# LayerNorm's mean product moved to the middle of a block of weight products; the last factors of the first 96 tokens in a PSUM bank of their own and multiplied first

## The chip, the core and the metric

The kernel runs on one core of one Trainium2 chip. The metric is the device time of one execution in microseconds. Three runs of the kernel before took 1078.56, 1078.71 and 1078.87 us, so the median is 1078.71 us.

A core has a matrix engine (PE in the profile, with its weight loads listed apart as PEld), three engines that work on elements (DVE, ACT, POOL), and an engine SP that here only issues transfers. Transfers are issued from the instruction streams ("queues") of SP, ACT and POOL. Every engine runs its own stream in order. An engine waits for another through semaphores. Products are written to PSUM, an accumulator memory divided into banks. Everything else lives in SBUF.

## What is computed

One layer of a decoder step for T = 288 tokens: 256 of a new sequence and 8 x 4 of running ones. The model width is D = 2048. Cut to what matters:

```
h   = rmsnorm(x)                       # 288 x 2048
a, gate, z = split(h @ w_in + b_in)    # three times 1024
c   = depthwise_conv31(a * sigmoid(gate)) + conv_b
c   = silu(layernorm(c) * ln_g + ln_b) # mean and variance over 1024
p   = (pooled(z) @ pool_w) * pool_scale
x   = x + concat(c, p) @ w_out
x   = x + relu(rmsnorm(x) @ w_ff1)**2 @ w_ff2    # width 8192
y   = rmsnorm(x)                       # the output
```

## The kernel before

Channels lie on the 128 partitions and tokens along the free dimension. A matrix product is cut into blocks of two output tiles of 128 channels, each 288 tokens wide in a PSUM tile `ac` with two banks. Because single matmuls run on rounded float32 values, each operand is split in a high part and a low part, and three of the four part products are taken. One block of `w_out` over eight input tiles (1024 inputs) is 8 x 2 x 3 = 48 matmuls.

The raw weights arrive in tiles `wr` of 128 x 1024 by transfers from SP. ACT writes the high part `whi` (L273). The low part `wlo` is the difference of raw and high part, taken by POOL in two pieces of 128 x 512 each (L281), or by DVE (L277), as a table says. For the `w_out` blocks it is POOL, for the later feed-forward blocks DVE. There are five buffers each for `whi` and `wlo`, so a cast L273 waits until PE has used up an earlier tile.

`gemm` (L309) issues the matmuls of a block; L304 is the one line that records every matmul. Its argument `between` names a function that is called at a given place among them: key `0` is ahead of the first matmul, key `4` is ahead of the pair of input tiles 4 and 5, which is half way through a block of eight. Its argument `classes` takes a string, `TURN`, by which the 48 matmuls of a block are put in another order; none is added or left out.

The pooling half of `w_out` runs first, in eight blocks g = 0 to 7 (L624 to L631). After each, DVE adds the result to `xT` (L631). Meanwhile DVE finishes the convolution's taps (L478), and then LayerNorm of the convolution's half is worked in between:

- `ln_mean` (L601): ACT copies a partial sum (L604), DVE adds the last tile to it (L605), and one PE product with a matrix of 1/1024 gives the mean in the PSUM tile `pmean`. It is called ahead of block g = 4.
- `ln_sums` (L608): DVE subtracts the mean from the four tiles `c` (L611, one operand in PSUM), ACT squares them (L613), DVE adds the four squares (three L617, then L618, all operands in SBUF). `by_parts` (L247) then splits the sum: ACT casts its high part (L251), DVE takes the low part into `hl` (L252), and PE multiplies both parts with a constant matrix. The result is the PSUM tile `norm`. It is called ahead of block g = 6.

Where no dependence forces an order, a scheduler decides where on each engine an instruction stands in the stream, from its own estimate of the times. It is not known from the program text alone.

At the end, the sum of squares of the final x is turned into one factor per token (L756 to L764). Three small products with an identity matrix spread 96 tokens each over all partitions (L767), once into the bank `ends` (`rows_f`) for DVE and once into `again`, which ACT copies to SBUF (`rf`, L779) for POOL. `finish` (L771) multiplies `xT` by the factors: DVE in six pieces of 1, 1, 2, 2, 3 and 3 tiles of 288 tokens, POOL in four pieces of one tile (L775). A transfer of each finished piece to the output follows at once (L776), in turn from SP and ACT.

The bank `idle` takes the results of three products that nothing reads (L759). They only keep PE running.

Of the kernel before, what the change touches and what calls it, by code (L numbers as in the profile page):

```python
# [12 lines left out]
ALU = mybir.AluOpType  # L13
# [3 lines left out]
P = 128  # L17
# [3 lines left out]
T = SEQ + NB * NS  # L21
TB = T // 3
# [47 lines left out]
TURN = "110100" * 4 + "01" * 6 + "1100" * 3  # L70
# [16 lines left out]
def trunk_kernel(ctx: ExitStack, tc: tile.TileContext, io):  # L87
# [3 lines left out]
    nc = tc.nc  # L91
# [14 lines left out]
    def nm(s):  # L106
        seen[s] = seen.get(s, 0) + 1
        return f"{s}{seen[s]}"
# [8 lines left out]
    def row(name):  # L117
        return rowp.tile([P, T], F32, name=nm(name), tag="row")
# [32 lines left out]
    xT = const.tile([P, KT, T], F32, name="xT")  # L151
# [63 lines left out]
    ident = const.tile([TB, TB], F32, name="ident", padded_shape=[TB, TB + 40])  # L215
# [85 lines left out]
    def mm(*args, **kw):  # L301

        with tc.issue_after(chain[-1]) if chain else nullcontext():
            last = nc.tensor.matmul(*args, **kw)  # L304
        if chain:
            chain[0] = last.ins
        return last

    def gemm(banks, rhs, added=None, m_outer=False, between={}, classes="", by_part=False, gets=None, pairs=None, late=0):  # L309


        n = len(rhs)
        gets = gets or ready.pop(0)
        todo, begins = [], {}
        if by_part:
            for k in range(0, n, 2):
                sets = [range(len(banks))] if k else [range(2), range(2, len(banks))]
                for last, ms_ in enumerate(sets, 1 - len(sets)):
                    for part, (w, x) in enumerate(((0, 0), (1, 0), (0, 1))):
                        if last == 0:  # L320
                            begins[len(todo)] = (k, None, k + 1)[part]
                        todo += [(k + (1 - d if x else d), m, w, x) for m in ms_ for d in range(2)]
        else:
            pairs = pairs or [(k, m) for k in range(0, n, 2) for m in range(len(banks))]
            if m_outer:
                pairs.sort(key=lambda km: km[1])
            for k, m in pairs:
                begins[len(todo)] = (k, m) if m else k
                todo += [(k + d, m, w, x) for d, w, x in ((0, 0, 0), (1, 0, 0), (0, 1, 0), (1, 1, 0), (1, 0, 1), (0, 0, 1))]
        todo[:late] = sorted(todo[:late], key=lambda p: p[2])  # L330
        head = todo[: len(classes)]
        for j, c in enumerate(classes):
            todo[j] = next(p for p in head if c == "." or (p[0] + p[3]) % 2 == int(c))
            head.remove(todo[j])
        if added:
            todo += [(n, 1, None, x) for x in range(2)]
        ends = {m: [f(j for j, p in enumerate(todo) if p[1] == m) for f in (min, max)] for m in range(len(banks))}
        ahead = None
        for j, (k, m, w, x) in enumerate(todo):
            if begins.get(j) in between:  # L340
                ahead = between[begins[j]]()
            with tc.issue_after(ahead.ins) if ahead is not None and not chain else nullcontext():
                last = mm(banks[m][:, :T], unit if w is None else gets[k // 8](k % 8, m)[w], added[x] if w is None else rhs[k][x], start=j == ends[m][0], stop=j == ends[m][1])
        ready.extend(itertools.islice(weights, 1))
        return last.ins

    def bank2():
        return acc.tile([P, 2, 512], F32, name=nm("ac"), tag="ac")

    def each(bk):  # L350
        return [bk[:, m, :] for m in range(2)]

    def halves(x2):

        return [(x2[0][:, m, :], x2[1][:, m, :]) for m in range(2)]
# [228 lines left out]
    proj = [halves(dd[k // 2])[k % 2] for k in korder]  # L584
# [34 lines left out]
        norm["rows"], last = row_of_sums(ssc[:, 0, :], "norm2", None, float(DC) / D, AF.Silu, parts=True)  # L619
        return last  # L620

    BETWEEN = {4: {0: ln_mean}, 6: {0: ln_sums}}
    behind = nullcontext()
    for g in range(8):  # L624
        bk = bks[g] if g < 2 else bank2()
        if g > 1:
            with behind:
                last = gemm(each(bk), proj, between=BETWEEN.get(g, {}), classes=TURN if g in (4, 6) else "")
        behind = tc.issue_after(last) if g > 3 else nullcontext()
        x2 = xT[:, 2 * g : 2 * g + 2, :]  # L630
        nc.vector.tensor_tensor(x2, x2, bk[:, :, :T], op=ALU.add)  # L631

    mixc = []
    for j, c in enumerate(cs):
        n = tmpp.tile([P, 2, T], F32, name=nm("n"), tag="ag", bufs=2)
# [17 lines left out]
    for g in range(8):  # L653
        bk = bks[g] if g < 2 else bank2()
        if g > 1:
            last = gemm(each(bk), mixc, classes=TURN if g == 2 else "")
# [14 lines left out]
        for m, (ah, al) in enumerate(a2):  # L671
            k = 2 * g + m
            xk = xT[:, k, :]
# [22 lines left out]
    for ch in range(DFF // FCH):  # L696
        fx, done = [], []
# [4 lines left out]
        for g in range(FCH // 256):  # L702
            bk = bank2()
# [4 lines left out]
            if ch or g:  # L708
# [9 lines left out]
                done = []  # L718
        last = ch == DFF // FCH - 1
        for g in range(8):  # L720
            bk = bank2()
# [7 lines left out]
            for m in range(2):  # L729
                k = 2 * g + m  # L730
                xk = xT[:, k, :]
# [19 lines left out]
    ends, again = ms("ends"), cvp.tile([P, 512], F32, name="again", tag="cv")[:, :T]  # L751
    sums_f, rows_f = ends[:TB, 0, 0:3], ends[:, 1, :T]
    idle = cvp.tile([P, 512], F32, name="idle", tag="cv")
    for n, (part, busy) in enumerate(((ssf, 0), (qf, 3))):
        for j in range(3):
            last = nc.tensor.matmul(sums_f[:, j : j + 1], part[:, j * TB : (j + 1) * TB], mean_d[:, 0:1], start=n + j == 0, stop=n == 1 and j == 2)  # L756
        with tc.issue_after(last.ins):
            for j in range(busy):
                nc.tensor.matmul(idle[:, 0:P], ones, ones, start=True, stop=True)  # L759
    root, first, s_f = [cst[:TB, 2 + 3 * j : 5 + 3 * j] for j in range(3)]  # L760
# [3 lines left out]
    nc.vector.scalar_tensor_tensor(out=s_f, in0=root, scalar=1.5, in1=first, op0=ALU.add, op1=ALU.mult)  # L764
    for spread_f in (rows_f, again):
        for j in range(3):
            nc.tensor.matmul(spread_f[:, j * TB : (j + 1) * TB], s_f[:, j : j + 1].to_broadcast([TB, P]), ident, start=j == 0, stop=j == 2)  # L767
    rf = row("rf")
    queues = (nc.sync, nc.scalar)

    def finish(eng, r, pieces):  # L771

        for j, (k0, n) in enumerate(pieces):
            xk = xT[:, k0 : k0 + n, :]
            eng.tensor_tensor(xk, xk, r[:, None, :].to_broadcast([P, n, T]), op=ALU.mult)  # L775
            queues[j % 2].dma_start(io["yT"][:, k0 : k0 + n, :], xk)  # L776

    finish(nc.vector, rows_f, ((0, 1), (1, 1), (2, 2), (4, 2), (6, 3), (9, 3)))
    nc.scalar.copy(rf, again)  # L779
    finish(nc.gpsimd, rf, [(k, 1) for k in range(12, KT)])  # L780


# [56 lines left out]
```

## Time and profile before

| | us |
|---|---|
| three runs: lowest, median, highest | 1078.56, 1078.71, 1078.87 |
| the profiled execution | 1078.44 |
| its span, first to last instruction | 1076.7 |
| PE busy | 1066.2 |
| DVE, ACT, POOL busy | 628.2, 482.2, 180.0 |

The profile is of one execution. Its span is 1.7 us shorter than its time; that rest lies outside the first and last instruction. A row of its timeline gives the start from the span's begin, the duration, the engine, the line and the operation, `out<-in` by the program's names, the shapes and a count when equal neighbours are merged (the duration then reaches from the first start to the last end). In brackets stands how long the engine was idle before, and what ended that. A name like SPq or ACTq is the engine's queue issuing a transfer. Matmuls are pipelined: two that follow each other at 0.13 us have a duration of 0.29 us each, and overlap.

### The profile page before, as it was taken

To read this page: it belongs to the slowest core of one execution; us is meant where nothing else is said; L and a number is where in the kernel's file an instruction comes from. 1 tells how busy PE (TensorE), PEld (TensorE's weight loads), DVE (VectorE), ACT (ScalarE), POOL (GpSimd) and SP (SyncE) were. 2 spreads that over 40 slices of the span, in tenths; PEclk is the share of its full clock that TensorE was granted. 3 is DMA by queue.
4 is the path that set the end of the run, shared out by engine and by line. 5 is a ranking of instruction groups with operands and counts; after the bars stand their busy time and mean duration, and the time that the engine had idled before them with its cause. 6 is when DMAs were issued, how large, how long until landed. Compare 5 with 4: busy or idle time off the path is not lost.

```text
span 1076.7 us, 19546 instructions
## 1 busy us (share of the span) xinstructions
PE 1066.2 (99%) x8176; PEld 1065.5 (99%) x8176; DVE 628.2 (58%) x799; ACT 482.2 (45%) x598; POOL 180.0 (17%) x192
## 2 busy tenths in 40 slices
PE   9999999999999999999999999999999999999996
PEld 9999999999999999999999999999999999999996
DVE  8899998878554544445554444455444445554553
ACT  8655654755544433334443333444433334444441
POOL 0989889423000000000000000000000000000001
PEclk9999999999999999999999999999999999999998
DMA  9897777555455555555545555555555555455522
GB/s 333 292 248 217 223 183 244 178 174 170 164 174 165 171 172 164 174 164 169 175 165 170 170 166 175 167 166 176 162 172 171 165 174 169 164 176 162 172 80 89
DMA packets 58873, 192.81 MB, mean 179 GB/s; under 512 B 6304, under 2 KB 11296, under 8 KB 58784
## 3 DMA queue, kind: packets, MB, share of 16 engines
q1 hardware_dynamic: 56336, 184.35, 52.6%
q0 software_dynamic: 1584, 5.77, 2.9%
q8 instruction: 64, 1.05, 0.4%
q10 hardware_dynamic: 864, 1.44, 0.4%
q14 instruction: 25, 0.20, 0.1%
HBM read 187.25 MB, written 4.28 MB: 178 GB/s over the span
## 4 chain that ended last, share of the span: by engine, by line
PE 79%; issue 20%; POOL 0%; DVE 0%; POOLq 0%
PE ac L304 78%; PE pp L304 1%; PE warm L214 1%; POOL xT L775 0%; POOLq L825 0%; DVE xT L748 0%; PE norm L304 0%; PE pmean L304 0%; PE mean L304 0%; DVE ones L204 0%; DVE cst L232 0%; POOLq L775 0%; DVE cst L231 0%
## 5 line engine op out<-in xcount | busy, mean ns | idle before, releaser
L273 ACT CAST whi<-wr 128x1024 fp32r<-128x1024 f32 (+1 forms) x332 | 346.4, 1043 | 541.5 <-PE ac L304 524.6
L277 DVE TENSOR_TENSOR wlo<-wr,whi 128x1024 fp32r<-128x1024 f32 x282 | 346.2, 1228 | 349.3 <-ACT whi L273 349.2
L304 PE MATMUL ac<-ax,whi 128*128 128x288 f32 x2048 | 351.1, 292 | 0.0
L304 PE MATMUL ac<-fx,whi 128*128 128x288 f32 x2048 | 350.2, 292 | 0.0
L304 PEld LDWEIGHTS ac<-ax,whi 128*128 128x128 f32 x2048 | 296.0, 187 | 0.0
L304 PEld LDWEIGHTS ac<-fx,whi 128*128 128x128 f32 x2048 | 295.7, 187 | 0.0
L304 PE MATMUL ac<-ax,wlo 128*128 128x288 f32 x1024 | 217.4, 292 | 0.0
L304 PE MATMUL ac<-fx,wlo 128*128 128x288 f32 x1024 | 216.4, 292 | 0.0
L304 PEld LDWEIGHTS ac<-ax,wlo 128*128 128x128 f32 x1024 | 162.6, 187 | 0.0
L304 PEld LDWEIGHTS ac<-fx,wlo 128*128 128x128 f32 x1024 | 162.3, 187 | 0.0
L775 POOL TENSOR_TENSOR xT<-xT,rf 128x288 f32<-128x288 f32 x4 | 3.1, 791 | 786.6 <-ACT rf L779 786.6
L304 PE MATMUL ac<-hx,whi 128*128 128x288 f32 x768 | 130.1, 293 | 0.0
L304 PEld LDWEIGHTS ac<-hx,whi 128*128 128x128 f32 x768 | 110.6, 187 | 0.2
L281 POOL TENSOR_TENSOR wlo<-wr,whi 128x512 fp32r<-128x512 f32 x78 | 104.3, 1394 | 19.9 <-ACT whi L273 17.4
L478 DVE SCALAR_TENSOR_TENSOR pc<-u_all,vec,pc 128x256 f32<-128x256 f32 x232 | 99.3, 481 | 5.0 <-ACT pc L475 3.6
L304 PE MATMUL ac<-hx,wlo 128*128 128x288 f32 x384 | 79.5, 292 | 0.0
L304 PEld LDWEIGHTS ac<-hx,wlo 128*128 128x128 f32 x384 | 60.3, 187 | 0.1
L304 PE MATMUL ac<-dx,whi 128*128 128x288 f32 x256 | 45.9, 294 | 0.0
L304 PE MATMUL ac<-mx,whi 128*128 128x288 f32 x256 | 44.5, 292 | 0.0
L711 DVE SCALAR_TENSOR_TENSOR t<-ac,r 128x576 f32<-128x576 f32 x32 | 24.2, 757 | 25.4 <-PE ac L304 25.3
L304 PEld LDWEIGHTS ac<-dx,whi 128*128 128x128 f32 x256 | 38.1, 188 | 0.1
L304 PEld LDWEIGHTS ac<-mx,whi 128*128 128x128 f32 x256 | 37.4, 187 | 0.0
(142 smaller groups left out, 541.8 us busy)
## 6 DMA issues: line engine op xcount, KB each, us to landing
wr<-in_w SPq DMA_DIRECT2D x335, 512.0 KB, 3.6
wlo<-in_w POOLq DMA_DIRECT2D x11, 512.0 KB, 9.3
xT<-in_xT SPq DMA_DIRECT2D x8, 288.0 KB, 7.3
wr<-in_w SPq DMA_DIRECT2D x5, 256.0 KB, 4.0
out_u_out<-u_all SPq DMA_DIRECT2D x1, 1208.0 KB, 8.9
u_all<-in_hist_c SPq DMA_DIRECT2D x8, 136.0 KB, 5.5
out_z_out<-z_all SPq DMA_DIRECT2D x1, 668.0 KB, 8.6
z_all<-in_hist_p SPq DMA_DIRECT2D x4, 152.0 KB, 6.9
```

The lines of the kernel that those rows point to most:

```text
L214: nc.tensor.matmul(warm[:, 0, 0:P], ones, ones, start=True, stop=True)
L273: nc.scalar.copy(hi, raw)
L277: nc.vector.tensor_tensor(lo, raw, f32(hi), op=ALU.subtract)
L281: nc.gpsimd.tensor_tensor(lo[:, j : j + 2, :], raw[:, j : j + 2, :], f32(hi[:, j : j + 2, :]), op=ALU.subtract)
L304: last = nc.tensor.matmul(*args, **kw)
L478: nc.vector.scalar_tensor_tensor(out=dst, in0=up[:, w : w + SEQ], scalar=cwv[:, w : w + 1], in1=pc, op0=ALU.mult, op1=ALU.add)
L711: nc.vector.scalar_tensor_tensor(out=t, in0=bk[:, :, :T], scalar=0.0, in1=both(rows2[0]), op0=ALU.max, op1=ALU.mult)
L775: eng.tensor_tensor(xk, xk, r[:, None, :].to_broadcast([P, n, T]), op=ALU.mult)
```

## The change

There are two edits.

In the `w_out` blocks, `ln_mean` is called at key 4 of block g = 4 in place of key 0, so its product stands behind 24 matmuls of that block. The order `TURN` is used for block 5 in place of block 4. Block 6 keeps it.

At the end, the product that spreads the first 96 tokens' factors goes to columns of the bank `idle` (`ahead_f`), not to `ends`. DVE multiplies these 96 tokens of four tiles first, then the other 192 tokens of the first pieces, then the 96 tokens of eight more tiles, then the rest. The transfers carry the same pieces from the same queues as before.

```diff
-    BETWEEN = {4: {0: ln_mean}, 6: {0: ln_sums}}
+    BETWEEN = {4: {4: ln_mean}, 6: {0: ln_sums}}
...
-                last = gemm(each(bk), proj, between=BETWEEN.get(g, {}), classes=TURN if g in (4, 6) else "")
+                last = gemm(each(bk), proj, between=BETWEEN.get(g, {}), classes=TURN if g in (5, 6) else "")
...
+    ahead_f = idle[:, P : P + TB]
...
     for spread_f in (rows_f, again):
         for j in range(3):
-            nc.tensor.matmul(spread_f[:, j * TB : (j + 1) * TB], s_f[:, j : j + 1].to_broadcast([TB, P]), ident, start=j == 0, stop=j == 2)
+            out = ahead_f if j == 0 and spread_f is rows_f else spread_f[:, j * TB : (j + 1) * TB]
+            nc.tensor.matmul(out, s_f[:, j : j + 1].to_broadcast([TB, P]), ident, start=j == 0 or out is not ahead_f and j == 1 and spread_f is rows_f, stop=j == 2 or out is ahead_f)
...
-    def finish(eng, r, pieces):
-
-        for j, (k0, n) in enumerate(pieces):
-            xk = xT[:, k0 : k0 + n, :]
-            eng.tensor_tensor(xk, xk, r[:, None, :].to_broadcast([P, n, T]), op=ALU.mult)
-            queues[j % 2].dma_start(io["yT"][:, k0 : k0 + n, :], xk)
-
-    finish(nc.vector, rows_f, ((0, 1), (1, 1), (2, 2), (4, 2), (6, 3), (9, 3)))
+    def times(eng, r, k0, n, t0=0):
+
+        xk = xT[:, k0 : k0 + n, t0 : t0 + r.shape[1]]
+        return eng.tensor_tensor(xk, xk, r[:, None, :].to_broadcast([P, n, r.shape[1]]), op=ALU.mult)
+
+    def finish(eng, r, pieces, t0=0, j0=0):
+
+        for j, (k0, n) in enumerate(pieces, j0):
+            done = times(eng, r, k0, n, t0)
+            queues[j % 2].dma_start(io["yT"][:, k0 : k0 + n, :], xT[:, k0 : k0 + n, :])
+        return done.ins
+
+    times(nc.vector, ahead_f, 0, 4)
+    last = finish(nc.vector, rows_f[:, TB:], ((0, 1), (1, 1), (2, 2)), TB)
+    with tc.issue_after(last):
+        times(nc.vector, ahead_f, 4, 8)
+    finish(nc.vector, rows_f[:, TB:], ((4, 2), (6, 3), (9, 3)), TB, 1)
```

PE's stream around the mean product, before: `ac_2473` is the result of block 3, `ac_2537` that of block 4, `dx_...` are the pooling half's inputs.

```order
 L304 MATMUL ac_2473<-dx_2119,wlo_2400 128x288 x2
 L304 MATMUL ac_2473<-dx_2119,whi_2399 128x288 x2
 L304 MATMUL pmean_2538<-sum_c,ones 128x288
 L304 MATMUL ac_2537<-dx_1242,whi_2462 128x288
 L304 MATMUL ac_2537<-dx_1242,wlo_2463 128x288
```

The same product in PE's stream now:

```order
 L304 MATMUL ac_2537<-dx_1582,wlo_2463 128x288 x2
 L304 MATMUL ac_2537<-dx_1582,whi_2462 128x288 x4
 L304 MATMUL ac_2537<-dx_1582,wlo_2463 128x288 x2
 L304 MATMUL ac_2537<-dx_1582,whi_2462 128x288 x2
 L304 MATMUL pmean_2562<-sum_c,ones 128x288
 L304 MATMUL ac_2537<-dx_1921,whi_2467 128x288 x2
 L304 MATMUL ac_2537<-dx_1921,wlo_2468 128x288 x2
```

It stands behind the block's first two input tile pairs (`dx_1242` and `dx_1582`), 24 matmuls later; the two products `norm` stay ahead of block 6.

DVE's stream from the last subtraction of the mean to `hl`; `ac_2537` is the result of block 4:

```order
-L611 TENSOR_TENSOR c_1716<-c_1716,pmean_2538 128x576
+L611 TENSOR_TENSOR c_636<-c_636,pmean_2562 128x576
+L611 TENSOR_TENSOR c_719<-c_719,pmean_2562 128x576
+L611 TENSOR_TENSOR c_1018<-c_1018,pmean_2562 128x576
+L611 TENSOR_TENSOR c_1716<-c_1716,pmean_2562 128x576
 L617 TENSOR_TENSOR q_2671<-q_2671,q_2674 128x576
+L631 TENSOR_TENSOR xT<-xT,ac_2537 128x576
 L617 TENSOR_TENSOR q_2671<-q_2671,q_2678 128x576
 L617 TENSOR_TENSOR q_2671<-q_2671,q_2682 128x576
 L618 TENSOR_TENSOR q_2671<-q_2671 128x288
-L631 TENSOR_TENSOR xT<-xT,ac_2537 128x576
 L252 TENSOR_TENSOR hl_2687<-q_2671,hl_2687 128x288
```

The addition of block 4's result (L631) has moved from behind L618 to between the first and the second addition of squares. The L611 rows differ only in the number of their tile.

ACT's stream over the same stretch; `whi_2599` belongs to block 6, `whi_2658` and `whi_2663` to block 7:

```order
 L273 CAST whi_2594<-wr_2590 128x1024
+L273 CAST whi_2599<-wr_2592 128x1024
 L613 ACTIVATE q_2671<-c_636 128x576
 L613 ACTIVATE q_2674<-c_719 128x576
 L613 ACTIVATE q_2678<-c_1018 128x576
-L273 CAST whi_2599<-wr_2592 128x1024
+L273 CAST whi_2658<-wr_2654 128x1024
 L613 ACTIVATE q_2682<-c_1716 128x576
-L273 CAST whi_2658<-wr_2654 128x1024
+L273 CAST whi_2663<-wr_2656 128x1024
 L251 CAST hl_2687<-q_2671 128x288
-L273 CAST whi_2663<-wr_2656 128x1024
```

Each of the three casts now stands one step of LayerNorm earlier. POOL's and SP's streams have the same rows in the same order as before, but for line numbers.

DVE's last rows now, in the place of six L775 rows on `ends` (two each of 128x288, 128x576 and 128x864):

```order
+L776 TENSOR_TENSOR xT<-xT,idle 128x4x96
+L776 TENSOR_TENSOR xT<-xT,ends_11504 128x192 x2
+L776 TENSOR_TENSOR xT<-xT,ends_11504 128x2x192
+L776 TENSOR_TENSOR xT<-xT,idle 128x8x96
+L776 TENSOR_TENSOR xT<-xT,ends_11504 128x2x192
+L776 TENSOR_TENSOR xT<-xT,ends_11504 128x3x192 x2
```

Two more rows read the first tokens' factors from `idle`, and the six rows on `ends` are 192 tokens wide per tile, not 288.

## The prediction

> **What bounds the kernel now.** I read the page first, then the chain of work that ended last, then PE's waits.
>
> ```profile
> span 1076.7 us, 19546 instructions
> PE 1066.2 (99%) x8176; PEld 1065.5 (99%) x8176; DVE 628.2 (58%) x799; ACT 482.2 (45%) x598; POOL 180.0 (17%) x192
> ...
> 188.56 0.51 PE pmean L304 x2
> 189.08 12.58 PE ac L304 x96
> 201.66 0.26 PE norm L304 x2
> 201.92 76.63 PE ac L304 x588
> ...
> PE ends L767 <- DVE cst L764: 0.2, 1, 0.2
> ```
>
> PE is busy for 1066.2 of 1076.7 us. From the first weights to the last block it waits for nothing: the list of its waits has one entry at the start and this one of 0.2 us in the tail. In the stretch that the change touches, the chain is PE from end to end: the mean product (two passes), blocks 4 and 5 (96 matmuls), the two `norm` products, and on. So whatever keeps PE waiting there is added to the time in full, and no other engine's work there can be shortened to any gain. Only the tail, where PE is through, can give something back.
>
> **The moved product itself.** It costs the same 0.51 us wherever it stands. Was it late before?
>
> ```profile
> 187.81 0.46 DVE L605 TENSOR_TENSOR sum_c<-pmean,c 128x288 f32<-128x288 f32 x1
> 188.60 0.75 DVE L631 TENSOR_TENSOR xT<-xT,ac 128x576 f32<-128x576 f32 x1 [0.34 <-PE ac L304]
> 189.27 2.74 DVE L611 TENSOR_TENSOR c<-c,pmean 128x576 f32<-128x576 f32 x4
> 191.93 3.91 DVE L617 TENSOR_TENSOR q<-q,q 128x576 f32<-128x576 f32 x3
> 195.88 1.43 DVE L618 TENSOR_TENSOR q<-q 128x288 f32<-128x288 f32 x1
> 197.23 0.74 DVE L631 TENSOR_TENSOR xT<-xT,ac 128x576 f32<-128x576 f32 x1
> 197.90 0.88 DVE L252 TENSOR_TENSOR hl<-q,hl 128x288 fp32r<-128x288 f32 x1
> ...
> 201.49 0.29 PE L304 MATMUL norm<-hl,means 128*128 128x288 f32 x1
> ```
>
> Its input L605 is done at 187.81 + 0.46 = 188.27, just ahead of its turn, and PE shows no wait. So the move takes away no stall: gain 0. Its other instructions, the copy L604 and L605, stand where they stood, and it issues no transfer. The order `TURN` goes from block 4 to block 5. Blocks 4 and 5 took 12.58 us for 96 matmuls, 0.131 each, against 76.63 / 588 = 0.130 later, so `TURN` costs under 0.1 us in either place. That the 24 matmuls behind the product now run in plain order is not in this trace; by the same two rates it is between 0 and 0.02 us.
>
> What changes is the time left behind it. Before, `hl` was ready at 197.90 + 0.88 = 198.78, and the first `norm` product ran at 201.49: 2.7 us to spare. The product now comes 24 x 0.13 = 3.1 us later, while `norm` keeps its place. **The slack is smaller than the delay**, so the chain from mean to `hl` has to be worked through.
>
> **How long that chain takes.** The rows for DVE above are uneven: L617 takes 0.76 us once and over 1.2 us twice, and L618, half as wide, takes 1.43. Single rows of DVE beside those of POOL show why.
>
> ```profile
> 191.32 1.28 POOL L281 TENSOR_TENSOR wlo<-wr,whi 128x512 fp32r<-128x512 f32 x1
> 191.93 1.28 DVE L617 TENSOR_TENSOR q<-q,q 128x576 f32<-128x576 f32 x1
> 193.32 0.76 DVE L617 TENSOR_TENSOR q<-q,q 128x576 f32<-128x576 f32 x1
> 193.52 1.70 POOL L281 TENSOR_TENSOR wlo<-wr,whi 128x512 fp32r<-128x512 f32 x1 [0.93 <-POOL wlo L281]
> 194.18 1.66 DVE L617 TENSOR_TENSOR q<-q,q 128x576 f32<-128x576 f32 x1
> 195.19 1.81 POOL L281 TENSOR_TENSOR wlo<-wr,whi 128x512 fp32r<-128x512 f32 x1
> 196.95 1.51 POOL L281 TENSOR_TENSOR wlo<-wr,whi 128x512 fp32r<-128x512 f32 x1
> ```
>
> POOL's piece ends at 192.60 and L617 0.61 later; the next pair ends at 195.22 and 195.84, 0.62 later. L618 ends 0.31 behind POOL's 197.00, and L252 0.32 behind its 198.46. The one L617 that found POOL idle took 0.76, and there POOL's piece was the longer one. So a DVE operation with both operands in SBUF and a POOL piece take turns. L611 and L631 read PSUM and keep 0.75 us throughout. The Trainium skill, "SBUF — State Buffer", section "SBUF: two separate sides", says it so: DVE with two SBUF inputs and GpSimd share a port pair, and whichever starts first holds it for its whole instruction. The rows agree.
>
> Now the chain is set on its new times. It needs ACT's rows, because POOL's pieces follow the casts.
>
> ```profile
> 192.34 1.05 ACT L273 CAST whi<-wr 128x1024 fp32r<-128x1024 f32 x1 [0.21 <-PE ac L304]
> 193.29 0.69 ACT L613 ACTIVATE q<-c 128x576 f32<-128x576 f32 x1
> 195.49 1.05 ACT L273 CAST whi<-wr 128x1024 fp32r<-128x1024 f32 x1 [1.52 <-issue]
> 197.34 0.43 ACT L251 CAST hl<-q 128x288 fp32r<-128x288 f32 x1 [0.80 <-DVE q L618]
> ```
>
> - The mean is there at 189.07 + 3.12 = 192.2. Four L611 (2.74) end at 194.9.
> - The cast at 192.34 waits for the first half of block 4, which now runs ahead of the product, 0.51 and a few hundredths earlier: 191.76. POOL began 193.52 - 192.34 = 1.18 behind the cast: now 192.94, and two pieces of 1.28 end at 195.5.
> - The first L617 is issued at 194.9 and loses its turn: 195.5 + 0.62 = 196.1.
> - L631, now second, ends at 196.1 - 0.08 + 0.75 = 196.77 (successors start 0.08 ahead of an end, as 197.23 against 197.31). The second L617 is issued at 196.69.
> - The cast at 195.49 waits for the end of block 4, which comes up to 0.1 earlier without `TURN`: 195.40. POOL's next piece begins 1.18 later: 196.58. The fourth L613 now stands behind this cast and ends by 195.40 + 1.05 + 0.69 = 197.1, in time for the third L617.
>
> So POOL would begin 0.1 us ahead of the second L617. **If POOL wins that turn**, its piece ends at 197.86 and L617 at 198.48. From there they alternate as before, when POOL's ends lay 1.78 (195.22 to 197.00) and 1.46 us (to 198.46) apart: POOL 199.64, third L617 200.26; POOL 201.42, L618 201.73; the cast L251 with 0.43 until 202.2; POOL 202.88, L252 at 203.20. The second `norm` product was due at 201.49 + 0.13 = 201.62. With 0.1 for handing over, PE waits 203.30 - 201.62 = **1.7 us**. This is also the worst of its kind: all five of DVE's operations then wait for the last five pieces that POOL has in this stage.
>
> Nothing hides this wait: PE runs in order, and block 6 is queued behind `norm`. What follows from `norm` shifts along with it.
>
> **The tail.** Which wait ends last there?
>
> ```profile
> 1066.00 0.91 PE L767 MATMUL ends<-ident,cst 96*128 96x96 f32 x6 [0.22 <-DVE cst L764]
> L775 DVE TENSOR_TENSOR xT<-xT,ends 128x576 f32<-128x576 f32 x2 | 1.4, 746 | 0.0
> L775 DVE TENSOR_TENSOR xT<-xT,ends 128x288 f32<-128x288 f32 x2 | 0.8, 450 | 1.0 <-PE ends L767 1.0
> 1066.94 0.46 DVE L775 TENSOR_TENSOR xT<-xT,ends 128x288 f32<-128x288 f32 x1 [1.00 <-PE ends L767]
> 1067.43 0.35 SPq L776 DMA_DIRECT2D out_yT<-xT  x1
> GB/s 0 0 0 0 0 0 0 0 0 0 0 0 0 0 0 0 0 0 0 173 377 182 412 374 423 396 366 447 407 363 445 401 407 347 41 11 0 0 0 0
> ```
>
> The last row cuts 1060 to 1077 into 40 slices of 0.425 us. The transfers run near 400 GB/s for all but two slices, the first (173) and the third (182). The end is bound by 16 x 144 KB of output, and only an earlier start and these gaps are to be had: at 400 GB/s, 0.24 + 0.23 us. One of three spreading products now lets DVE begin: two passes of 0.91 / 6 on, with the first start, near 1066.5, not 1066.94. The multiplication of 4 x 96 tokens is not in the trace: it lies between 450 ns (288 elements) and 746 (576), by the line between them 550. A 192-token piece is by the same line near 350. The first transfer is then issued at 1066.5 + 0.55 + 0.35 - 0.08 = 1067.3, against 1067.43: 0.1 us earlier. The third piece comes 0.4 earlier, but the 8 x 96 tokens (by the line 0.95 us) then delay the fourth by 0.3 and open a gap there. Together I take 0.2 us, with bounds of 0 and 0.5.
>
> **Sum.** The profiled execution took 1078.44; + 1.7 - 0.2 = 1079.9. The median of the three runs lies 0.27 above it, so the forecast for a median is **1080.2 us**, 1.5 us or 0.14% slower. A measurement of this kernel tells apart from no change about 0.2%, 2.2 us, so this counts as no difference.
>
> **Rivals.** First: DVE wins the turn at 196.7. The start of a row need not be the moment at which the port is taken:
>
> ```profile
> 127.19 1.89 POOL L281 TENSOR_TENSOR wlo<-wr,whi 128x512 fp32r<-128x512 f32 x1
> 127.23 0.70 DVE L524 SCALAR_TENSOR_TENSOR d<-s,z_all 128x512 f32<-128x512 f32 x1
> 231.54 0.91 POOL L682 TENSOR_TENSOR ss<-ss,q 128x288 f32<-128x288 f32 x1
> 231.70 1.06 DVE L675 SCALAR_TENSOR_TENSOR ax<-xT,vec,ax 128x288 fp32r<-128x288 f32 x1
> ```
>
> With a lead of 0.04 POOL lost and was stretched to 1.89; with 0.16 it won. The lead of 0.1 lies between. By the skill's rule above, POOL wins with any lead, which the first pair contradicts. If DVE wins, L617 ends at 197.45, POOL 1.15 later (as 195.22 behind 194.08) at 198.60, and the same alternation gives `hl` at 202.2: a wait of 0.7 us, a median of 1079.2.
>
> Second: the chain fits after all, for one POOL piece less in the way. Then only the tail is left: 1078.5. Against it: without any turn lost behind the first, the chain would still take three L617 or L631 of 0.75, 0.45 for L618 and a cast.
>
> Third, on the slower side: the wait lets PE's clock drop.
>
> ```profile
> 1070.00:1071.00 1.00, 0.00 (x0) 0.00 (x0) 1.00 (x2) 0.00 (x0) 1.00 (x2) 1.00 1.06 396
> 1071.00:1072.00 1.00, 0.00 (x0) 0.00 (x0) 0.02 (x1) 0.00 (x0) 0.15 (x1) 0.63 1.08 411
> ```
>
> The third number from the right is the granted clock: full up to 1071, more than 3 us after the last spreading products, then falling. A wait of 1.7 us is about half of that, so the point is not reached. If it were, a clock at half for some 3.4 us would add 1.7 (an estimate): 1081.9. "TensorE: Matmul & The Clock Gate" of the Trainium skill, part 1, gives an idle window of about 3.4 us, free-running; the rows agree that the drop comes after more than 3 us.
>
> **How the numbers follow.** POOL wins the turn, 0.50: 1079.8 to 1080.6. DVE wins it, 0.28: 1078.8 to 1079.5. No wait, 0.10: 1078.2 to 1078.8. The clock drops or something else unseen is late, 0.10: 1081 to 1083. A gain by a path that I do not see, 0.02. Faster by over 0.2% would need 2.2 us where only the tail's 0.5 is to be had: 0.02. Slower by over 0.2% is 0.12, the fourth case and the edge of the first. The range is 1078.5 to 1080.9.
>
> **What would show it.** Right: PE waits on `norm` for DVE's `hl`, 0.7 or 1.7 us; L617 and L618 end 0.6 and 0.3 behind POOL's pieces; DVE's first multiplication near 1066.5 plus the wait. Wrong: no wait of PE at `norm`, `hl` ready before 201.6, or another order of POOL and DVE at the second L617.

## The result and the profile after

| | median, us | lowest, us | ratio to before, with its 95% interval |
|---|---|---|---|
| before (14 executions) | 1078.86 | 1078.44 | |
| changed (14 executions) | 1080.76 | 1080.14 | 1.0018 [1.0011, 1.0025] |
| changed, second set (11) | 1081.26 | 1080.20 | 1.0016 [1.0007, 1.0025] |

The change makes the kernel slower by some 0.17%, about 1.8 us. One execution of the first set took 1252.14 us at a granted clock of 0.79; the ratio leaves it out, and without it that set's median is 1080.57. Both intervals lie above 1, and they are narrower than the 0.2% that the forecast took as the resolution: the loss is small, but it is measured. The profile after is of an execution of the second set, of 1080.93 us with a span of 1079.2 us.

PE's list of waits in the changed kernel (us in total, times, longest), without the 1.1 us at the start that both kernels have:

```profile
PE norm L304 <- ACT hl L251: 0.6, 1, 0.6
PE norm L304 <- DVE hl L252: 0.6, 1, 0.6
PE ac L304 <- DVE hx L368: 0.4, 1, 0.4
PE idle L769 <- DVE cst L765: 0.2, 1, 0.2
```

PE now waits twice at `norm`, once for each half of `hl`. The third row is a wait at the program's first block. In the traces of this case it lies between 0 and 1.3 us, though the programs are the same up to there, so it is not put down to the change.

The chain that ended last shows the detour. It was PE from end to end in this stretch; now it leaves PE at the mean product and comes back at `norm` (start, duration, what):

```profile
167.44 25.05 PE ac L304 x192
192.50 0.50 PE pmean L304 x2
193.00 0.02 issue
193.02 2.75 DVE c L611 x4
195.77 1.16 DVE q L617
...
197.51 1.88 DVE q L617
...
199.48 1.69 DVE q L617
...
201.19 1.44 DVE q L618
...
202.66 0.44 ACT hl L251
...
203.12 0.96 DVE hl L252
204.08 0.04 issue
204.13 0.40 PE norm L304
204.53 25.58 PE ac L304 x196
```

The list of waits gives 1.2 us, but what PE lost is read from starts, since ends of matmuls are modelled. PE's timeline around `norm`:

```profile
202.21 0.29 PE L304 MATMUL ac<-dx,whi 128*128 128x288 f32 x1
203.14 0.40 PE L304 MATMUL norm<-hl,means 128*128 128x288 f32 x1 [0.64 <-ACT hl L251]
204.13 0.40 PE L304 MATMUL norm<-hl,means 128*128 128x288 f32 x1 [0.58 <-DVE hl L252]
204.36 0.29 PE L304 MATMUL ac<-dx,whi 128*128 128x288 f32 x1
```

From the last matmul of block 5 to the first of block 6 it is 204.36 - 202.21 = 2.15 us. Three steps at 0.13 would be 0.39, as before. **PE lost 1.76 us here.** Single rows of POOL and DVE show the turns:

```profile
197.47 1.30 POOL L281 TENSOR_TENSOR wlo<-wr,whi 128x512 fp32r<-128x512 f32 x1 [1.16 <-ACT whi L273]
197.51 1.87 DVE L617 TENSOR_TENSOR q<-q,q 128x576 f32<-128x576 f32 x1
198.72 1.82 POOL L281 TENSOR_TENSOR wlo<-wr,whi 128x512 fp32r<-128x512 f32 x1
199.48 1.68 DVE L617 TENSOR_TENSOR q<-q,q 128x576 f32<-128x576 f32 x1
200.56 1.75 POOL L281 TENSOR_TENSOR wlo<-wr,whi 128x512 fp32r<-128x512 f32 x1
202.27 1.49 POOL L281 TENSOR_TENSOR wlo<-wr,whi 128x512 fp32r<-128x512 f32 x1
```

POOL's piece began 0.04 us ahead of the second L617 and kept the port. L617 ended 0.61 behind it (198.77 and 199.38), the third L617 0.62 behind the next (200.54 and 201.16), L618 0.31 behind the one after (202.31 and 202.62).

In the tail, three of DVE's groups by form, and from the timeline the first transfer:

```profile
L776 DVE TENSOR_TENSOR xT<-xT,idle 128x768 f32<-128x768 f32 x1 | 0.9, 947 | 0.0
L776 DVE TENSOR_TENSOR xT<-xT,ends 128x192 f32<-128x192 f32 x2 | 0.6, 348 | 0.0
L776 DVE TENSOR_TENSOR xT<-xT,idle 128x384 f32<-128x384 f32 x1 | 0.6, 554 | 0.6 <-PE idle L769 0.6
```

```profile
1069.95 0.35 SPq L782 DMA_DIRECT2D out_yT<-xT  x1
```

DVE now waits 0.6 us for its factors, not 1.0. The durations are those of the line through 450 and 746 ns. Counted from the end of the factors' last step, the first transfer is issued after 1.40 us, 1.48 before, and the last output lands after 9.63, 9.75 before: 0.12 us gained. Single executions differ here by nearly as much: seven of the eight traces used here with this tail have 9.62 to 9.73, and one (key 6, below) has 9.94; the two traces with the old tail have 9.75 and 9.78.

### The profile page after: what moved, and what is told of

The parts are those of the page before. It is cut to its first block, busy times and chain, and to the rows that moved or that the text cites. A ratio compares the mean times of both kernels' runs of the same rounds, so it can differ in the third digit from the quotient of the medians.

```text
span 1250.4 us, 19548 instructions
## 1 busy us (share of the span) xinstructions
PE 1240.1 (99%) x8176; PEld 1239.0 (99%) x8176; DVE 630.6 (50%) x801; ACT 482.5 (39%) x598; POOL 177.1 (14%) x192
## 4 chain that ended last, share of the span: by engine, by line
PE 80%; issue 19%; DMA 0%; POOL 0%; DVE 0%; POOLq 0%; ACT 0%
PE ac L304 79%; PE pp L304 1%; DMA wr<-in_w 0%; POOL xT L776 0%; PE norm L304 0%; POOLq L836 0%; DVE xT L748 0%; PE pmean L304 0%; ACT whi L365 0%; DVE hx L368 0%; PE mean L304 0%; DVE wlo L374 0%; POOLq L776 0%
## 5 line engine op out<-in xcount | busy, mean ns | idle before, releaser
L304 PE MATMUL ac<-ax,whi 128*128 128x288 f32 x2048 | 397.1, 320 | 0.0
L304 PE MATMUL ac<-fx,whi 128*128 128x288 f32 x2048 | 389.9, 317 | 0.0
L304 PEld LDWEIGHTS ac<-ax,whi 128*128 128x128 f32 x2048 | 330.9, 196 | 0.0
L304 PEld LDWEIGHTS ac<-fx,whi 128*128 128x128 f32 x2048 | 325.2, 195 | 0.0
L304 PE MATMUL ac<-ax,wlo 128*128 128x288 f32 x1024 | 242.7, 320 | 0.0
L304 PE MATMUL ac<-fx,wlo 128*128 128x288 f32 x1024 | 238.6, 316 | 0.0
L304 PEld LDWEIGHTS ac<-ax,wlo 128*128 128x128 f32 x1024 | 178.8, 198 | 0.0
L304 PEld LDWEIGHTS ac<-fx,wlo 128*128 128x128 f32 x1024 | 176.9, 198 | 0.0
L304 PE MATMUL ac<-hx,whi 128*128 128x288 f32 x768 | 154.7, 332 | 0.2 <-DVE hx L368 0.2
L304 PEld LDWEIGHTS ac<-hx,whi 128*128 128x128 f32 x768 | 130.1, 200 | 0.4 <-issue 0.3
```

## Experiments

Each edit is against the changed kernel unless it says otherwise. Each run has its own median, and a ratio to the kernel before, run beside it. The theory: DVE and POOL take turns at an SBUF port, which makes the chain from the mean to `hl` too long for a later mean product. In the expectations it is theory 1 where POOL wins the turn at the second L617, and theory 2 where DVE does. The rows show the turns; that a port is behind them is the prediction's reading. The rivals: the change costs by the pace of PE's matmuls, by any place of the product inside the block, or in the tail.

### The changed kernel again

No edit.

> The changed kernel once more, for a profile at full clock. Theory 1 (DVE and POOL take turns at the port, POOL wins the turn near 196.7): PE waits about 1.7 us at the second norm product for DVE's hl, L617 and L618 end 0.6 and 0.3 us behind POOL's pieces, time 1.4 to 1.7 us over before. Theory 2 (DVE wins that turn): wait 0.7 us, time 0.5 us over before. Rival (PE's pace): no wait at norm; the 24 matmuls behind the mean product or the blocks without TURN run slower than 0.131 us each, and that makes the difference. Tail: DVE's first multiplication 0.25 us after the factors' last step plus spreading of 0.56, first transfer 0.1 us earlier than before, end 0 to 0.5 us nearer to the factors.

Median 1081.26 us; its profile is shown above. Theory 1 holds: a loss of 1.76 us at `norm`, with DVE's ends where they were expected. PE's pace is not the cause: from the first matmul of block 4 or the mean product, whichever comes first, to the last of block 5 it took 12.965 us before and 12.998 now, 0.03 more.

This execution was also late before it came to the change. The chain's row for the products `norm` of the first stage, before and now:

```profile
33.37 0.48 PE norm L304 x2
```

```profile
34.18 0.48 PE norm L304 x2
```

That is 0.81 us, and no more is lost from there to block 4. With the change, 0.81 + 1.76 + 0.03 - 0.12 = 2.48 us; the two profiled executions are 1080.93 - 1078.44 = 2.49 apart.

### Each edit alone

The first run is the kernel before with the first edit:

```diff
-    BETWEEN = {4: {0: ln_mean}, 6: {0: ln_sums}}
+    BETWEEN = {4: {4: ln_mean}, 6: {0: ln_sums}}
...
-                last = gemm(each(bk), proj, between=BETWEEN.get(g, {}), classes=TURN if g in (4, 6) else "")
+                last = gemm(each(bk), proj, between=BETWEEN.get(g, {}), classes=TURN if g in (5, 6) else "")
```

The second is the changed kernel with these two lines put back.

> The first edit alone (mean product at the middle of block 4, TURN on block 5), the tail as before. Theory 1: the whole of the loss is here, 1.7 us over before, with the same wait at norm as the full change. Theory 2: 0.7 us over. Rival: the loss is in the tail, and this kernel is within 0.2 us of before.

> The second edit alone, mean product and TURN as before. Theories 1 and 2: no wait at norm, 0.2 us under before (0 to 0.5), which the timing may not resolve. Rival (the tail loses): 1 us or more over before.

The first edit alone has a median of 1080.72 us, ratio 1.0018 [1.0009, 1.0026], and loses the same 1.76 us at `norm`. The tail alone has 1079.11, ratio 0.9998 [0.9989, 1.0007]; its PE does not wait at `norm`, and its last output lands 9.66 us behind the factors. So the whole loss belongs to the first edit. The tail's 0.1 us is seen in the trace and is below what the times resolve.

### The same place, but without turns

The sum of squares is taken up in PSUM, so DVE never has both operands in SBUF. The mean product stays where the change put it.

```diff
...
+        total = cvp.tile([P, 512], F32, name="total", tag="cv")[:, :T]
...
+            if j == 0:
+                nc.scalar.activation(total, c[:, 0, :], AF.Square)
+                nc.scalar.activation(q[:, 1, :], c[:, 1, :], AF.Square)
             else:
-                nc.vector.tensor_tensor(ssc, ssc, q, op=ALU.add)
-        nc.vector.tensor_tensor(ssc[:, 0, :], ssc[:, 0, :], ssc[:, 1, :], op=ALU.add)
...
+                nc.scalar.activation(q, c, AF.Square)
+            for m in range(0 if j else 1, 2):
+                nc.vector.tensor_tensor(total, total, q[:, m, :], op=ALU.add)
...
```

> The full change, with LayerNorm's sum of squares taken up in PSUM: the first half of the first square is written to PSUM by ACT, and DVE adds the other seven halves to it one by one (7 operations of 128x288, about 0.46 us each, one operand in PSUM), in place of three L617 and L618 with both operands in SBUF. Same position of the mean product. Theory 1 and 2 (turns at the port make the chain long): no DVE operation waits for a POOL piece, hl is ready near 199.4, PE does not wait at norm, time 0.2 us under before. Rival (the wait comes from the later mean product alone, or from PE's pace): the time stays 1 us or more over before.

Median 1078.79 us, ratio 1.0000 [0.9991, 1.0009]. DVE's timeline, and POOL's over the same stretch:

```profile
195.22 0.46 DVE L619 TENSOR_TENSOR total<-total,q 128x288 f32<-128x288 f32 x1
...
196.41 3.10 DVE L619 TENSOR_TENSOR total<-total,q 128x288 f32<-128x288 f32 x6
200.34 0.46 DVE L252 TENSOR_TENSOR hl<-total,hl 128x288 fp32r<-128x288 f32 x1 [0.83 <-ACT hl L251]
...
197.00 2.55 POOL L281 TENSOR_TENSOR wlo<-wr,whi 128x512 fp32r<-128x512 f32 x2 [1.16 <-ACT whi L273]
200.09 2.55 POOL L281 TENSOR_TENSOR wlo<-wr,whi 128x512 fp32r<-128x512 f32 x2 [0.54 <-ACT whi L273]
```

DVE does the sums in seven operations, not four, and still `hl` is ready 8.93 us behind the start of the mean product, not 11.74 (10.38 before). The execution was 0.35 us late at block 4; on the clock of before `hl` came at 200.45, 1.0 us later than expected, among other things because ACT's cast L251 stood behind a weight cast. Neither engine's operations are stretched: POOL's pairs take 2.55, twice the 1.28 of a free piece, while DVE works beside them. PE does not wait at `norm`. So the later product costs nothing when no turn is in the chain. That chain is also shorter than the one before, which had turns of its own. Had the chain kept its 10.38 us, the changed kernel would still have lost about 0.3 us at `norm` (an estimate: its second `norm` product was due 10.14 us behind the start of the mean product, and it follows `hl` by 0.05). The other 1.5 us or so come from the longer chain. How much of that is due to the addition L631, which now stands between two L617, and how much to POOL's pieces alone, no run separates.

### The delay halved, and half as large again

```diff
-    BETWEEN = {4: {4: ln_mean}, 6: {0: ln_sums}}
+    BETWEEN = {4: {2: ln_mean}, 6: {0: ln_sums}}
```

The second run has key 6 in place of 2.

> The full change with the mean product 12 matmuls into block 4, not 24 (the delay halved to 1.6 us). Turns at the port: the chain from the mean to hl has 1.1 us less than the spare 2.7 us used up by the delay, and one or two turns more than before; hl is ready near 201.5 of before's clock, PE waits 0 to 0.2 us, time 0.1 us under to 0.1 over before. Rival (any place inside the block costs, since the product then stands among matmuls): about the same loss as the full change, 1.5 us or more.

> The full change with the mean product 36 matmuls into block 4 (the delay half as large again, 4.7 us). Turns at the port: POOL has two pieces of block 7's first tile and two of its second left for four of DVE's five operations, the last one runs free; PE waits 2.6 us at norm, 0.9 us more than the full change though the product comes 1.6 us later; time 2.5 us over before. Rival (a plain shift of the chain by the delay): 1.6 us more than the full change, 3.2 us over before.

The scheduler moved L631 in both: it stands behind the second L617 with key 2, and ahead of the first with key 6. So these runs change more than the delay.

With half the delay, PE does not wait: median 1079.23 us, ratio 1.0005 [0.9996, 1.0015].

```profile
201.26 0.46 DVE L252 TENSOR_TENSOR hl<-q,hl 128x288 fp32r<-128x288 f32 x1 [0.50 <-ACT hl L251]
```

`hl` is ready at 201.72, and the `norm` products start at 201.85 and 201.99, so next to nothing was left of the slack. The rival, that any place inside the block costs, has no support here: from block 4 to behind `norm` PE lost 0.08 us against before.

With the larger delay, the median is 1084.46, ratio 1.0052 [1.0037, 1.0067], from four executions. PE's timeline at `norm`, its other wait, and the chain on two later stretches of one execution:

```profile
203.20 0.29 PE L304 MATMUL ac<-dx,whi 128*128 128x288 f32 x1
205.97 0.89 PE L304 MATMUL norm<-hl,means 128*128 128x288 f32 x2 [2.48 <-ACT hl L251]
206.70 0.29 PE L304 MATMUL ac<-dx,whi 128*128 128x288 f32 x1
```

```profile
PE ac L304 <- DMA wlo<-in_w: 0.6, 1, 0.6
```

```profile
57.88 24.13 PE ac L304 x181
...
89.94 18.08 PE ac L304 x139
```

At `norm` PE lost 206.70 - 203.20 - 0.39 = 3.11 us, where 2.6 was expected and 3.2 by a plain shift: the expectation missed, and the rival's number came out. The last DVE operation was free (0.46 us), as the theory has it, but one of POOL's pieces waited 0.58 us for its cast and started later than assumed. The rest of the loss is elsewhere: a transfer came late near 52 us, and from there PE ran at 24.13 / 181 = 133 ns per matmul, until the next block in the order `TURN`, behind which it runs at 18.08 / 139 = 130. Why all four counted executions were so slow, though the program ahead of the stage is the same, stays open.

### The order TURN left on block 4

```diff
-                last = gemm(each(bk), proj, between=BETWEEN.get(g, {}), classes=TURN if g in (5, 6) else "")
+                last = gemm(each(bk), proj, between=BETWEEN.get(g, {}), classes=TURN if g in (4, 6) else "")
```

> The full change with TURN left on block 4 (and none on block 5): the mean product at the same place. Turns at the port: the same wait at norm within 0.1 us, 1.6 us over before. Rival (the order of matmuls behind the product matters): a time clearly under that of the full change, back at before's.

Median 1079.32 us, ratio 1.0006 [0.9997, 1.0015]: the expected 1.6 us did not come. POOL and DVE at the turn, and PE at `norm`:

```profile
198.78 0.75 DVE L617 TENSOR_TENSOR q<-q,q 128x576 f32<-128x576 f32 x1
198.79 1.88 POOL L281 TENSOR_TENSOR wlo<-wr,whi 128x512 fp32r<-128x512 f32 x1 [1.21 <-ACT whi L273]
203.70 0.29 PE L304 MATMUL norm<-hl,means 128*128 128x288 f32 x1
204.27 0.40 PE L304 MATMUL norm<-hl,means 128*128 128x288 f32 x1 [0.28 <-DVE hl L252]
```

DVE began 0.01 us ahead of POOL, won, and took 0.75; now POOL's piece is the long one. The loss at `norm` is 0.55 us, not 1.76. Nothing else changed in the streams but the order of matmuls in two blocks. So the rival (the order matters) came out by its time, but not by its mechanism: blocks 4 and 5 themselves ran 0.14 us slower. The order only moved the turn by some 0.05 us, and one turn is worth 1.2 us. In the trace that is 0.55 + 0.14 = 0.69 us; lowest against lowest, this kernel is 1079.10 - 1078.39 = 0.7 us over before, so the turn in the profiled execution is no exception.

### PE's pace behind a wait

The runs above showed PE at 133 ns behind waits. Two runs take `TURN` off block 6, right behind `norm`, once with the wait and once without (sums in PSUM).

```diff
-                last = gemm(each(bk), proj, between=BETWEEN.get(g, {}), classes=TURN if g in (5, 6) else "")
+                last = gemm(each(bk), proj, between=BETWEEN.get(g, {}), classes=TURN if g == 5 else "")
```

> The full change without TURN on block 6, the block right behind the wait at norm (plain order there; every matmul stays). Earlier runs show PE at 133 ns per matmul, not 130, after a wait or behind the mean product, until a block in the order TURN. If PE keeps that slower pace after a wait: blocks 6 and 7 and the 96 matmuls behind them run at about 133 ns, until the next TURN some 24 us later, 192 x 3 ns = 0.6 us, so 0.5 us over the full change. Rival (the pace recovers by itself): 130 ns in block 7, time within 0.1 us of the full change.

> The same without TURN on block 6, with the sums of squares in PSUM, so that PE does not wait at norm. If the wait sets the slower pace: 130 ns in blocks 6 and 7, time of the PSUM variant. If the two inserted norm products set it: 133 ns as in the other kernel, 0.5 us over the PSUM variant.

The chain between 212 and 218 us, first with the wait, then without:

```profile
211.99 6.14 PE ac L304 x46
```

```profile
211.94 6.11 PE ac L304 x47
```

6.14 / 46 is 133.5 ns, 6.11 / 47 is 130.0. The wait sets the slower pace, the inserted products don't, and it lasts: the 144 matmuls from the third of block 6 on took 19.19 us with the wait and 18.72 without it, 133.3 and 130.0 ns each. In the trace the expected 0.5 us is there: from the first matmul of block 6, 300 steps took 39.71 us, and 39.18 in the changed kernel. In time the first run is not told apart from the changed kernel (median 1081.03 us, ratio 1.0017 [1.0008, 1.0027]). The second has 1078.48, ratio 0.9997 [0.9987, 1.0007].

### A tail without the lull, and the best of all parts

```diff
-        times(nc.vector, ahead_f, 4, 8)
-    finish(nc.vector, rows_f[:, TB:], ((4, 2), (6, 3), (9, 3)), TB, 1)
+        last = times(nc.vector, ahead_f, 4, 2).ins
+    with tc.issue_after(last):
+        last = finish(nc.vector, rows_f[:, TB:], ((4, 2),), TB, 1)
+    with tc.issue_after(last):
+        times(nc.vector, ahead_f, 6, 6)
+    finish(nc.vector, rows_f[:, TB:], ((6, 3), (9, 3)), TB, 0)
```

This is on the kernel with the tail alone changed.

> The second edit alone, with the 8 x 96 tokens cut in two: 2 tiles ahead of the fourth piece, 6 tiles behind it. The fourth piece's transfer is then issued 0.6 us earlier than in the changed tail (2.9 us behind the factors, not 3.46), the lull of the transfers near it goes, and the last output lands 0.1 to 0.2 us nearer to the factors than with the changed tail (9.5 us, not 9.65; before 9.75). In time 0.2 us under before, which the timing may not resolve. Rival (the end is set by the last POOL piece and its transfer): the lull goes but the last landing stays at 9.65.

What the transfers moved in 40 slices of the same 10.2 us (GB/s), with the tail of the change and then with this one:

```profile
GB/s 0 0 0 0 0 0 0 0 126 379 371 443 398 398 271 375 249 407 398 357 393 457 420 393 434 312 447 402 434 407 352 348 281 18 9 9 0 0 0 0
```

```profile
GB/s 0 0 0 0 0 0 0 0 226 380 393 420 407 407 416 389 416 375 371 384 466 407 420 420 335 447 420 366 434 343 371 240 18 9 9 0 0 0 0 0
```

The lull (271 and 249) is gone, and the last output lands 9.43 us behind the factors, against 9.66 and 9.75. The median is 1078.47, ratio 0.9997 [0.9988, 1.0007].

Last, this tail with the LayerNorm of before and no `TURN` on block 6, where nothing waits.

> The kernel before in its LayerNorm (mean product ahead of block 4, TURN on block 4), with TURN taken off block 6, where PE does not wait, and with the tail of the run with the 8 x 96 tokens cut in two. By the traces: 0.3 us less from factors to last landing, 0.1 us less in block 6; 0.4 us under before, 1078.3 us where before has 1078.7. Rival (the inserted norm products set the slower pace after all): blocks 6 and 7 at 133 ns, 0.5 us more, and no gain.

Median 1079.18 us, ratio 1.0000 [0.9991, 1.0009]: no gain that can be measured. In the trace the parts are there (9.44 us to the last landing; 130 ns in block 6). But in the profiled execution a weight load (PEld) waited 0.2 us for a late transfer near 101 us, and behind it the chain shows the slower pace:

```profile
PEld ac L304 <- DMA wlo<-in_w: 0.2, 1, 0.2
```

```profile
109.89 24.13 PE ac L304 x181
```

That is 133 ns again, up to the blocks near 168 us that are issued in another order (`TURN` behind 24 matmuls). On the way there PE fell back another 1.6 us against the kernel before. What the edits save is smaller than what such an execution loses, so none of these kernels is shown to beat the one before.

## Why the prediction was right

- **The moved product gains nothing.** Blocks 4 and 5 with the product took no less than before, so no stall was taken away. The cost of `TURN` and plain order, put at under 0.1 and 0 to 0.02 us, measured 0.03 together.
- **The slack is smaller than the delay.** 2.7 against 3.1 us, and the wait is at `norm` for `hl`. With half the delay it is gone, with the turns taken out it is gone. But this step alone is worth only some 0.3 us; the longer chain is the rest.
- **Five operations in turns, 1.7 us.** Measured 1.76 at full delay. The row-by-row working held to about 0.1 us: `hl` was put at 203.20, and came at 204.07 - 0.81 = 203.26 on the same clock.
- **Who wins the turn.** POOL was put 0.1 us ahead; it was 0.04 to 0.05 ahead, and won, in the traces of this kernel, of the first edit alone and of the run without `TURN` on block 6. The forecast took the right branch on a margin thinner than it knew, and that part is luck. The pair quoted for the rival, where POOL lost with a lead of 0.04, does not hold here. When the order of matmuls shifted the turn by 0.05, the rival's branch came true, at 0.55 us instead of its 0.7.
- **The tail.** 0.2 us was taken, with bounds of 0 and 0.5; it measured 0.12 in the trace shown, and the times do not resolve it. The step that was mis-sized is the gap at the fourth piece, which was named but hardly counted: cutting the 8 x 96 tokens in two brought 0.2 us more.
- **The time.** Lowest against lowest, the loss is 1080.14 - 1078.44 = 1.7 us; the terms give 1.76 + 0.03 - 0.12 = 1.67. The median came out at 1080.76, over the forecast by 0.56 and inside the range's upper end by 0.14; at 1080.57 it is 0.37 over. The forecast allowed 0.27 for the spread between executions. The profiled ones show where more comes from: a start that is up to 0.8 us late, late transfers, and the pace behind them. The other executions have no trace, so for them this stays open.
- **The clock** stayed at 1.00 through a wait of 2.5 us at `norm` (key 6), so the slow rival's point was not reached.
- **The resolution** was put at 0.2%. The intervals came out at 0.07 to 0.1% to either side (0.15% with key 6), so a loss of this size can be told from none.

## What to carry to other kernels

Before a step is moved later, count the slack at the place that needs its result, and rebuild the chain between with the durations of that very stage, not with the shortest of their kind. Where DVE and POOL took turns, an operation of 128x288 that is 0.46 us long when free cost 1.43; keeping one operand in PSUM took such operations out of the queue. A forecast that hangs on 0.05 us between two engines should be given as two branches.

## What the runs showed of the hardware that was not expected

After a wait, PE does not come back to its pace by itself. Before it, matmuls of 128x288 start every 130.0 ns; behind it every 133.3, over hundreds of matmuls, at a granted clock of 1.00. It returns to 130.0 behind a block whose matmuls are issued in the order `TURN`. Behind the two passes of the mean product the pace is much the same: 132.9 over the 24 matmuls in plain order. A run without a wait at the same place kept 130.0. So a short wait early in the program can cost more than itself until the next such block: 0.8 us lost at a late transfer cost 0.8 more in the run with key 6, and 0.2 cost 1.6 more in the last run. What in PE holds this state, the runs do not show.
